# Neighbourhood attention: the products with v take the context's part first and the second head first

## Chip, cores and metric

The kernel runs on one core of one Trainium2 chip. The metric is device time of one execution in microseconds (us); three executions of the kernel before gave 3345.22, 3346.32 and 3348.22 us, median 3346.32. A second, profiled execution gives the trace from which every other time here is read.

## Reference

The program is a trunk of two layers over 1024 latent tokens (a grid of 16 rows by 64 columns) and 256 context tokens, width 1024. Layer 0 is a recurrent and a convolutional mixer, then an MLP. Layer 1, the one that is changed, is neighbourhood attention with 16 heads of width 64, then an MLP. For each grid row of queries:

```python
s_lat = jnp.einsum('bhqd,bhkd->bhqk', q_r, k_blk).astype(f32) + bias.astype(f32)
s_lat = jnp.where(blk_mask, s_lat, -jnp.inf)
s_ctx = jnp.einsum('bhqd,bhkd->bhqk', q_r, kc).astype(f32)
p = jax.nn.softmax(jnp.concatenate([s_lat, s_ctx], axis=-1), axis=-1).astype(v.dtype)
return (jnp.einsum('bhqk,bhkd->bhqd', p[..., :nk], v_blk)
        + jnp.einsum('bhqk,bhkd->bhqd', p[..., nk:], vc))
```

One softmax runs over the window's keys and all context keys; its weights are multiplied with the window's v and with the context's v, and the two products are added.

## The kernel before

Layer 1 works through eight **head pairs** (hp 0 to 7). `natten_proj` projects a pair's q, k and v from the normed activations: long chains of 128x512 products (L177 to L179, tiles psg), a sum of squares per head on TensorE (L902, tile psn), and a normalisation on ACT and DVE (tiles n). `natten_attn` then does the pair's attention in four **column blocks** (`cb`), and in each block for both heads (`hh`):

1. Scores: for each of two halves of the rows (`rb`) a product with the context's keys into the tile `pc` and one with the window's keys into a tile `p_`, each split into a high and a low part (L978, L979, tiles psf). One head needs three PSUM tiles of tag "f".
2. Softmax: DVE takes the maximum over the context part (L982), adds the bias `TM` and finishes the maximum (L984, twice), negates it (L986); ACT exponentiates (L989, L990, twice); DVE adds and inverts the sums (L96 st, L992) and scales (L994, twice).
3. Transposes of the weights on TensorE (L999 for each half's window part, L1006 for the context part) into one PSUM tile of tag "m", each evacuated before the next may start: L999 by ACT into tiles `s` (L1001), L1006 by DVE into a tile `pc` in SBUF (L1008).
4. When both heads are there, twenty products with v into one PSUM tile `po` (L1014 with the window's v `Vw`, L1018 with the context's `Vc`). Head 0 writes partitions 0 to 63 and head 1 partitions 64 to 127, so each uses half of the array's columns ("128*64" in the trace, where other products are "128*128"). `po` is copied out by ACT (L1192) and stored.

Buffers are few, which matters for the order. PSUM has three banks for tag "f" (scores and `po`), three for "g" (projections), one for "m" and one for "n":

```python
PS3 = dict(g=3, f=3, m=1, n=1)
```

The low part of q, `Ql`, has three buffers for the two heads of two pairs, and the next pair's second one is cleared on GpSimd (L897) when the pair's first head has read its own for the last time:

```python
Ql = [mk(nl, [P, LAT], "Ql", 3, F32R) for _ in range(2)]
for hh in range(2):
    G.memset(Ql[hh][64 - 64 * hh:128 - 64 * hh].bitcast(F32), 0.0)
```

Nothing of the order on an engine is written by hand. A scheduler fixes it before the run: attention has a high priority (`na=500`), and the next pair's projection fills TensorE in between. On the chip each engine runs its list strictly in that order, so an instruction that has to wait holds up all that stand behind it. Products that add into the same tile keep the order of the program.

Of the kernel before, what the change touches and what calls it, by code (L numbers as in the profile page):

```python
# [27 lines left out]
def kernel(ctx: ExitStack, tc: tile.TileContext, A, out):  # L28
    nc = tc.nc
    V, S, T, G = nc.vector, nc.scalar, nc.tensor, nc.gpsimd  # L30
# [8 lines left out]
    def mk(pool, shape, tag, bufs, dt=F32):  # L39
        cnt[0] += 1  # L40
        return pool.tile(shape, dt, tag=tag, bufs=bufs, name=f"{tag}_{cnt[0]}")
# [18 lines left out]
    def pr(k):  # L60
        k = HP.get(k, k)
        return ExitStack() if k is None else tc.high_priority(k)
# [13 lines left out]
    def pt(shape, tag):  # L76
        cnt[0] += 1
        return psp[0].tile(shape, F32, tag=tag, bufs=psp[1][tag], name=f"ps{tag}_{cnt[0]}")
# [7 lines left out]
    def s2(shape=None):  # L86
        return mk(base, shape or [P, 512], "s2", 4)
# [10 lines left out]
    def add(o, a, b):  # L98
        return tt(o, a, b, ALU.add)
# [845 lines left out]
    def natten_attn(hp, qkv, ap_, nl, store):  # L945
        with pr("na"):
            Q, Ql, Kt, vT = qkv
            vl = vT[:, 0:LAT].rearrange("p (r c) -> p r c", c=64)

            def tokens(src, n, tag):  # L950

                ps = pt([P, 4, P], TV)
                for i in range(n):
                    T.transpose(ps[:, i], src[:, i * P:(i + 1) * P], ident)
                o = mk(ap_, [P, n, P], tag, 2)
                S.copy(o, ps[:, :n])
                return o

            Vc = tokens(vT[:, LAT:NT], 2, "Vc")
            for cb in range(4):  # L960
                ct = (0, 1, 1, 2)[cb]
                vs = mk(ap_, [P, 512], "vs", 1)
                G.tensor_copy(vs.rearrange("p (r c) -> p r c", c=32), vl[:, :, KC0[cb]:KC0[cb] + 32])
                Vw = tokens(vs, 4, "Vw")
                pT = []
                for hh in range(2):
                    TM = mk(nl, [P, 2, 384], "TM", 2)
                    nc.gpsimd.dma_start(TM, A["rpbT"][2 * hp + hh, ct])
                    kl = Kt[hh][:, 0:LAT].rearrange("p (r c) -> p r c", c=64)
                    pc = pt([P, 2, CTX], "f")  # L970
                    st = mk(ap_, [P, 8], "st", 6)
                    pw, pe = [], []
                    for rb in range(2):
                        c0 = rb * 512 + cb * P
                        p_ = pt([P, 512], "f")
                        for o, kx in ((pc[:, rb], Kt[hh][:, LAT:NT]),
                                      (p_[:, :384], kl[:, 4 * rb:4 * rb + 12, KC0[cb]:KC0[cb] + 32])):
                            T.matmul(o, Q[hh][:, c0:c0 + P], kx, start=True, stop=False)  # L978
                            T.matmul(o, Ql[hh][:, c0:c0 + P], kx, start=False, stop=True)  # L979
                        pw.append(p_)  # L980
                        pe.append(mk(ap_, [P, 640], "pe", 4))
                    V.tensor_reduce(out=st[:, 0:2], in_=pc, axis=AX.X, op=ALU.max)  # L982
                    for rb in range(2):
                        V.tensor_tensor_reduce(out=pe[rb][:, 0:384], in0=pw[rb][:, :384], in1=TM[:, rb], scale=1.0, scalar=st[:, rb:rb + 1],  # L984
                                               op0=ALU.add, op1=ALU.max, accum_out=st[:, 2 + rb:3 + rb])
                    V.tensor_scalar(out=st[:, 2:4], in0=st[:, 2:4], scalar1=-1.0, scalar2=None, op0=ALU.mult)  # L986
                    for rb in range(2):
                        e = pe[rb]
                        S.activation(e[:, 0:384], e[:, 0:384], AF.Exp, bias=st[:, 2 + rb:3 + rb], accum_out=st[:, 4 + rb:5 + rb])  # L989
                        S.activation(e[:, 384:640], pc[:, rb], AF.Exp, bias=st[:, 2 + rb:3 + rb], accum_out=st[:, 6 + rb:7 + rb])  # L990
                    add(st[:, 4:6], st[:, 4:6], st[:, 6:8])
                    V.reciprocal(st[:, 4:6], st[:, 4:6])  # L992
                    for rb in range(2):
                        V.tensor_scalar(out=pe[rb], in0=pe[rb], scalar1=st[:, 4 + rb:5 + rb], scalar2=None, op0=ALU.mult)  # L994
                    tw = []
                    for rb in range(2):
                        ps = pt([P, 4, P], (TA, TB)[rb])
                        for j in range(3):
                            T.transpose(ps[:, j], pe[rb][:, j * P:(j + 1) * P], ident)  # L999
                        w_ = s2([P, 3, P])  # L1000
                        S.copy(w_, ps[:, 0:3])  # L1001
                        tw.append(w_)
                    ps = pt([P, 2, 2, P], TC)
                    for rb in range(2):
                        for j in range(2):
                            T.transpose(ps[:, j, rb], pe[rb][:, 384 + j * P:512 + j * P], ident)  # L1006
                    tc_ = mk(ap_, [P, 2, 2, P], "pc", 2)
                    V.tensor_copy(tc_, ps)  # L1008
                    pT.append((tw, tc_))
                po = pt([P, 2, P], PO)  # L1010
                for rb in range(2):
                    for j in range(3):
                        for hh in range(2):
                            T.matmul(po[64 * hh:64 * hh + 64, rb], Vw[:, rb + j, 64 * hh:64 * hh + 64],  # L1014
                                     pT[hh][0][rb][:, j], start=(j == 0), stop=False)
                    for j in range(2):
                        for hh in range(2):
                            T.matmul(po[64 * hh:64 * hh + 64, rb], Vc[:, j, 64 * hh:64 * hh + 64],  # L1018
                                     pT[hh][1][:, j, rb], start=False, stop=(j == 1))
                store(cb, po)  # L1020


# [162 lines left out]
    with tc.tile_pool(name="nl", bufs=1, reuse_waits="tile") as nl, \  # L1185
# [3 lines left out]
        def store(hp):  # L1189
            def f(cb, po):  # L1190
                o = mk(nl, [P, 2, P], "o", 1)
                S.copy(o, po)  # L1192
                nc.gpsimd.dma_start(od[hp, :, :, cb], o)
            return f

        for hp in range(7):
            natten_attn(hp, natten_proj(hp, h, na, nl, cst, *([OR] if hp == 0 else [])), na, nl, store(hp))
# [4 lines left out]
        def direct(cb, po):  # L1202
            for g in range(2):
                hi, lo = blkd(g, 7)
                split(hi[:, cb], lo[:, cb], po[:, g].rearrange("p (r q) -> p r q", q=16))

        natten_attn(7, qkv, na, nl, direct)
        xg = [mk(hpool[0], [P, 8, 512], "h2", 1)]
        nc.sync.dma_start(xg[0], xs[:, :, 0:512])
# [158 lines left out]
```

## Time and profile before

| | us |
|---|---|
| median of three executions | 3346.32 |
| profiled execution, whole | 3341.84 |
| span of its trace | 3340.1 |
| attention of layer 1 in the trace, first product with v to last | 1958.1 to 2561.2 |

The page of the profile gives each engine's busy time and the chain of work that ended last. The timeline lists an engine's instructions in order of time: start, length, engine, line, tile, how many were merged, and in brackets how long the engine stood idle before them and for what. A product's length includes the passage through the array, which overlaps the next product, so the cost of one is the distance between starts. A product with v is recorded as two passes: 640 products stand as 768 + 512 records.

### The profile page before, as it was taken

Reading aid. Unit: us, or ns where it says so; the run is one execution under the profiler, and the core shown is the slowest. Engines: PE = TensorE matmul, PEld = TensorE weight load, DVE = VectorE, ACT = ScalarE, POOL = GpSimd, SP = SyncE. Lnnn points to the kernel's source line nnn. Section 1 sums busy time; section 2 is a strip of 40 time slices with the busy share of each in tenths; the row PEclk is TensorE's granted clock in tenths of the full one; section 3 lists DMA queues with packets and bytes.
Section 4 is the critical chain, followed back from the end, with each engine's and each line's share of the span. In section 5 each row is a group of like instructions: output and inputs, shape, how many; then the busy total and the mean of one; then the engine's idle time right before and its main releaser. Section 6 shows DMA issues by size and latency. Waiting matters only on the chain.

```text
span 3340.1 us, 45203 instructions
## 1 busy us (share of the span) xinstructions
PE 3232.4 (97%) x18044; PEld 2637.5 (79%) x18044; DVE 2056.8 (62%) x3790; ACT 1200.4 (36%) x2539; POOL 96.5 (3%) x160
## 2 busy tenths in 40 slices
PE   7799999999999999999999999999999999999999
PEld 4678887778877888888888777777777788888887
DVE  4958997556684444544445877666666754455454
ACT  5742221343442212111121576666664422121111
POOL 0000000000000000000000011111110000000000
PEclk9899999999999999999999999999999999999999
DMA  6432224776522212121111221222234111111111
GB/s 208 163 110 67 81 73 146 231 241 208 189 97 95 70 57 89 57 89 64 51 45 32 79 69 59 70 64 70 67 96 144 65 62 46 49 51 47 48 45 70
DMA packets 140876, 306.11 MB, mean 92 GB/s; under 512 B 12497, under 2 KB 74057, under 8 KB 139258
## 3 DMA queue, kind: packets, MB, share of 16 engines
q1 hardware_dynamic: 131018, 266.60, 24.5%
q0 software_dynamic: 6464, 28.84, 2.8%
q10 hardware_dynamic: 3184, 7.78, 0.7%
q8 instruction: 142, 2.33, 0.3%
q14 instruction: 68, 0.56, 0.1%
HBM read 255.93 MB, written 43.05 MB: 90 GB/s over the span
## 4 chain that ended last, share of the span: by engine, by line
PE 77%; DVE 8%; DMA 3%; ACT 2%; issue 1%; SPq 0%; ACTq 0%; DVEq 0%
PE psg L177 13%; PE psg L178 13%; PE psg L179 13%; PE psf L313 8%; PE psf L312 8%; PE psf L314 8%; DMA wm<-in_w_mod 3%; PE psf L1014 2%; PE psm L999 1%; DVE b L96 1%; PE psf L978 1%; PE psf L979 1%; DVE n L108 1%; DVE q L96 1%; PE psf L1018 1%; PE psm L218 1%
## 5 line engine op out<-in xcount | busy, mean ns | idle before, releaser
L177 PE MATMUL psg<-h,wh 128*128 128x512 f32 (+1 forms) x2728 | 1014.8, 372 | 13.5 <-ACT h L289 7.1
L179 PE MATMUL psg<-h,wl 128*128 128x512 f32 (+1 forms) x2728 | 1003.9, 368 | 5.7 <-DVE wl L113 5.4
L178 PE MATMUL psg<-h,wh 128*128 128x512 f32 (+1 forms) x2728 | 1007.9, 370 | 1.0 <-DVE h L108 0.9
L177 PEld LDWEIGHTS psg<-h,wh 128*128 128x128 f32 x2728 | 516.5, 189 | 109.4 <-issue 17.3
L179 PEld LDWEIGHTS psg<-h,wl 128*128 128x128 f32 x2728 | 516.2, 189 | 93.4 <-DVE wl L113 10.6
L178 PEld LDWEIGHTS psg<-h,wh 128*128 128x128 f32 x2728 | 516.3, 189 | 91.7 <-issue 14.2
L108 DVE SCALAR_TENSOR_TENSOR x<-psf,modT,x 128x512 f32<-128x512 f32 (+1 forms) x512 | 347.1, 683 | 218.8 <-PE psf L314 218.7
L313 PE MATMUL psf<-al,w2h 128*128 128x512 f32 (+1 forms) x1280 | 471.6, 369 | 0.6 <-DVE al L113 0.6
L314 PE MATMUL psf<-ah,w2l 128*128 128x512 f32 (+1 forms) x1280 | 470.9, 368 | 0.0
L312 PE MATMUL psf<-ah,w2h 128*128 128x512 f32 (+1 forms) x1280 | 468.6, 369 | 0.1
L112 ACT CAST w2h<-w2r 128x1024 fp32r<-128x1024 f32 x64 | 67.3, 1051 | 765.9 <-PE psf L313 595.9
L113 DVE TENSOR_TENSOR wl<-wr,wh 128x1024 fp32r<-128x1024 f32 (+2 forms) x144 | 172.9, 1200 | 213.3 <-ACT wh L112 212.7
L312 PEld LDWEIGHTS psf<-ah,w2h 128*128 128x128 f32 x1280 | 240.4, 188 | 44.4 <-ACT ah L112 2.6
L313 PEld LDWEIGHTS psf<-al,w2h 128*128 128x128 f32 x1280 | 241.2, 189 | 43.3 <-DVE al L113 2.3
L314 PEld LDWEIGHTS psf<-ah,w2l 128*128 128x128 f32 x1280 | 241.2, 188 | 40.4 <-issue 0.5
L112 ACT CAST wh<-wr 128x1024 fp32r<-128x1024 f32 (+2 forms) x144 | 148.4, 1031 | 249.2 <-PE psg L178 207.6
L108 DVE SCALAR_TENSOR_TENSOR rr<-psg,rr 128x512 f32<-128x512 f32 x160 | 101.3, 633 | 176.6 <-ACT rr L301 176.6
L113 DVE TENSOR_TENSOR w2l<-w2r,w2h 128x1024 fp32r<-128x1024 f32 x64 | 78.2, 1222 | 151.6 <-ACT w2h L112 149.9
L301 ACT ACTIVATE rr<-psg 128x512 f32<-128x512 f32 x160 | 88.0, 550 | 194.7 <-PE psg L179 193.3
L113 DVE TENSOR_TENSOR al<-rr,ah 128x512 fp32r<-128x512 f32 x160 | 101.8, 636 | 84.1 <-ACT ah L112 84.1
L112 ACT CAST ah<-rr 128x512 fp32r<-128x512 f32 x160 | 92.4, 578 | 170.0 <-DVE rr L108 170.0
L108 DVE SCALAR_TENSOR_TENSOR h<-psf,modT,h 128x512 f32<-128x512 f32 x128 | 94.2, 747 | 44.2 <-PE psf L314 44.2
(286 smaller groups left out, 4046.2 us busy)
## 6 DMA issues: line engine op xcount, KB each, us to landing
wm<-in_w_mod SPq DMA_DIRECT2D x96, 512.0 KB
wr<-in_w SPq DMA_DIRECT2D x64, 512.0 KB
w2r<-in_w SPq DMA_DIRECT2D x64, 512.0 KB
big<-d SPq DMA_DIRECT2D x39, 640.0 KB
TM<-in_rpbT POOLq DMA_DIRECT2D x64, 384.0 KB, 3.4
wr<-in_w_in SPq DMA_DIRECT2D x29, 512.0 KB
wr<-in_w_qkv SPq DMA_DIRECT2D x24, 512.0 KB
d<-b SPq DMA_DIRECT2D x8, 1280.0 KB
```

The lines of the kernel that those rows point to most:

```text
L96: return (e or V).tensor_tensor(out=o, in0=a, in1=b, op=op)
L108: return V.scalar_tensor_tensor(out=o, in0=a, scalar=s, in1=b, op0=op0, op1=op1)
L112: S.copy(hi, x)
L113: (e or V).tensor_tensor(out=lo, in0=x, in1=hi.bitcast(F32), op=ALU.subtract)
L177: T.matmul(ps[:M, :n], hi[:, k, :M], hh[g][:, k, :n], start=(i == 0), stop=False)
L178: T.matmul(ps[:M, :n], hi[:, k, :M], hl[g][:, k, :n], start=False, stop=False)
L179: T.matmul(ps[:M, :n], lo[:, k, :M], hh[g][:, k, :n], start=False, stop=(i == len(ks) - 1))
L301: S.activation(r[:, :n], ps[:, :n], AF.Relu)
L312: T.matmul(ps[:, :n], w2h[:, d], ah[g], start=(i == 0), stop=False)
L313: T.matmul(ps[:, :n], w2h[:, d], al[g], start=False, stop=False)
L314: T.matmul(ps[:, :n], w2l[:, d], ah[g], start=False, stop=(i == 1))
L1014: T.matmul(po[64 * hh:64 * hh + 64, rb], Vw[:, rb + j, 64 * hh:64 * hh + 64], pT[hh][0][rb][:, j], start=(j == 0), stop=False)
```

## The change

The two loops of each `rb` change places, and the heads are visited as (1, 0):

```diff
                 for rb in range(2):
+                    for j in range(2):
+                        for hh in (1, 0):
+                            T.matmul(po[64 * hh:64 * hh + 64, rb], Vc[:, j, 64 * hh:64 * hh + 64],
+                                     pT[hh][1][:, j, rb], start=(j == 0), stop=False)
                     for j in range(3):
-                        for hh in range(2):
+                        for hh in (1, 0):
                             T.matmul(po[64 * hh:64 * hh + 64, rb], Vw[:, rb + j, 64 * hh:64 * hh + 64],
-                                     pT[hh][0][rb][:, j], start=(j == 0), stop=False)
-                    for j in range(2):
-                        for hh in range(2):
-                            T.matmul(po[64 * hh:64 * hh + 64, rb], Vc[:, j, 64 * hh:64 * hh + 64],
-                                     pT[hh][1][:, j, rb], start=False, stop=(j == 1))
+                                     pT[hh][0][rb][:, j], start=False, stop=(j == 2))
```

The same twenty products per block remain. The context's products are L1014 in the kernel after and L1018 in the kernel before, the window's the other way round. The first product now needs the second head's transposed context weights, the last tile that a block makes.

The scheduler's order changes with it, on TensorE from the first block of hp 0 to the end of hp 7. The first place is TensorE at the third block of hp 5 (scores of the block after it are psf_20735 and psf_20737). Before, the first product with v stands alone, between the first head's transposes and the next block's scores:

```order
L999 MATMUL psm_20640<-ident,pe_20621 128x128 x3
L1014 MATMUL psf_20700<-s_3713_20638,Vw_20604 64x128
L978 MATMUL psf_20735<-KK_20025,Q_20019 128x256
L979 MATMUL psf_20735<-KK_20025,Ql_20021 128x256
L978 MATMUL psf_20735<-KK_20025,Q_20019 128x256
L979 MATMUL psf_20735<-KK_20025,Ql_20021 128x256
L179 MATMUL psg_20960<-h_1650_8777,wl_20957 128x512
L177 MATMUL psg_20960<-h_1650_8777,wh_20956 128x512
L1006 MATMUL psm_20646<-ident,pe_20615 128x128 x2
```

Five more of that block's products follow with one of the context's behind the second head's L999, and thirteen more behind its L1006. After, the block's twenty stand together directly behind the second head's L1006; these are the first of them:

```order
L1006 MATMUL psm_20693<-ident,pe_20662 128x128 x2
L1006 MATMUL psm_20693<-ident,pe_20668 128x128 x2
L1014 MATMUL psf_20700<-pc_20698,Vc_20341 64x128
L1014 MATMUL psf_20700<-pc_20651,Vc_20341 64x128
L1014 MATMUL psf_20700<-pc_20698,Vc_20341 64x128
L1014 MATMUL psf_20700<-pc_20651,Vc_20341 64x128
L1018 MATMUL psf_20700<-s_3726_20685,Vw_20604 64x128
```

What moved: in each of the 32 blocks three runs of 1, 6 and 13 products became one run of 20, and the scores of the next block, which stood between those runs, now stand behind the run.

The second place is TensorE right behind that run, in the fourth block of the same pair. After, all sixteen score products of both heads come first (the last eight of them are shown), then one L902 and the first head's transposes, and only then a projection product:

```order
L978 MATMUL psf_20782<-KK_20026,Q_20020 128x256
L979 MATMUL psf_20782<-KK_20026,Ql_20022 128x256
L978 MATMUL psf_20784<-KK_20026,Q_20020 128x384
L979 MATMUL psf_20784<-KK_20026,Ql_20022 128x384
L978 MATMUL psf_20790<-KK_20026,Q_20020 128x384
L979 MATMUL psf_20790<-KK_20026,Ql_20022 128x384
L902 MATMUL psn_21029<-n_3793_21027,bd_8340 128x512
L999 MATMUL psm_20761<-ident,pe_20742 128x128 x3
L999 MATMUL psm_20767<-ident,pe_20748 128x128 x3
L177 MATMUL psg_21092<-h_1650_8777,wh_21088 128x512
```

Before, the first head's scores of that block had been issued a block earlier, and projection products stand in front of its transposes:

```order
L978 MATMUL psf_20790<-KK_20026,Q_20020 128x384
L979 MATMUL psf_20790<-KK_20026,Ql_20022 128x384
L179 MATMUL psg_21002<-h_1652_8779,wl_20957 128x512
L177 MATMUL psg_21002<-h_1652_8779,wh_20956 128x512
L178 MATMUL psg_21002<-h_1653_8780,wh_20956 128x512
L179 MATMUL psg_21002<-h_1652_8779,wl_20957 128x512
L177 MATMUL psg_21002<-h_1652_8779,wh_20956 128x512
L178 MATMUL psg_21002<-h_1653_8780,wh_20956 128x512
L999 MATMUL psm_20761<-ident,pe_20742 128x128 x3
```

What moved: the scores of the first head went from before the third block's products with v to behind them, and six projection products that stood between the scores and the transposes are gone from there. The same piece of order, with other tile numbers, stands in hp 0 to hp 6.

The third place is DVE at that same fourth block, where st_20736 is the first head's statistics and Ql_20854 the next pair's second `Ql`. After:

```order
L982 TENSOR_REDUCE st_20736<-psf_20735 128x2
L96 TENSOR_TENSOR Ql_20854<-n_3778_20896,Q_20852 64x512
L984 ISA pe_20742,st_20736<-psf_20737,TM_20733,st_20736 128x384
L984 ISA st_20736 128x1
L984 ISA pe_20748,st_20736<-psf_20743,TM_20733,st_20736 128x384
L984 ISA st_20736 128x1
L96 TENSOR_TENSOR Ql_20854<-n_3783_20940,Q_20852 64x512
L986 TENSOR_SCALAR st_20736<-st_20736 128x2
```

Before, both L984 stand ahead of the first write of Ql_20854, with other work between:

```order
L984 ISA pe_20748,st_20736<-psf_20743,TM_20733,st_20736 128x384
L984 ISA st_20736 128x1
L96 TENSOR_TENSOR Ql_20854<-n_3778_20896,Q_20852 64x512
L986 TENSOR_SCALAR st_20736<-st_20736 128x2
L108 SCALAR_TENSOR_TENSOR n_3783_20940<-psg_20910,gain_8344,n_3783_20940 128x512
```

What moved: the write of Ql_20854, which must wait for GpSimd's clearing and so for the first head's last score product, went ahead of the two L984 of that head.

## Prediction

> **What bounds the kernel now.** I read the page first, then the stage of the attention by windows, then its timeline.
>
> ```profile
> PE 3232.4 (97%) x18044; PEld 2637.5 (79%) x18044; DVE 2056.8 (62%) x3790; ACT 1200.4 (36%) x2539; POOL 96.5 (3%) x160
> ...
> core 0: us, PE busy (x) PEld busy (x) DVE busy (x) ACT busy (x) POOL busy (x), PEclk, DMA share, GB/s
> ...
> 1995.00:2003.00 8.00, 5.44 (x39) 3.40 (x33) 6.79 (x17) 6.09 (x17) 2.63 (x4) 1.00 0.40 126
> 2003.00:2500.00 497.00, 493.45 (x3290) 387.99 (x3290) 342.07 (x767) 327.34 (x820) 73.40 (x111) 1.00 0.22 68
> 2500.00:2562.00 62.00, 58.34 (x401) 44.76 (x402) 42.84 (x98) 34.25 (x91) 4.01 (x7) 0.94 0.48 155
> ```
>
> TensorE (PE) is the bound: in the 497 us of hp 1 to 6 it stands idle for 3.55 us. DVE and ACT are busy for 69% and 66% of it and set nothing there, because projection products always stand between an attention step and the next one that needs its result. Two stretches are different: in hp 0 (1995 to 2003) a third of PE's time is idle, and hp 7 loses 3.7 us. So the change matters in two ways only: what it takes from PE's own work, and whether PE still has something to do while a softmax runs.
>
> **What it removes: changes of the array's shape.** The products with v use half of the columns. Around a run of them the timeline of PE shows a gap:
>
> ```profile
> 2286.95 0.55 PE L999 MATMUL psm<-ident,pe 128*128 128x128 f32 x3
> 2287.43 0.76 PE L1014 MATMUL psf<-s,Vw 128*64 128x128 f32 x9
> 2287.92 0.27 PE L1018 MATMUL psf<-pc,Vc 128*64 128x128 f32 x1
> 2288.03 0.27 PE L1014 MATMUL psf<-s,Vw 128*64 128x128 f32 x1
> 2288.03 0.27 PE L1018 MATMUL psf<-pc,Vc 128*64 128x128 f32 x1
> 2288.24 0.39 PE L979 MATMUL psf<-KK,Ql 128*128 128x256 f32 x1
> 2288.46 0.40 PE L177 MATMUL psg<-h,wh 128*128 128x512 f32 x1
> ...
> 2289.83 0.34 PE L978 MATMUL psf<-KK,Q 128*128 128x384 f32 x1
> 2290.00 0.34 PE L979 MATMUL psf<-KK,Ql 128*128 128x384 f32 x1
> ...
> 2291.95 0.66 PE L954 MATMUL psm<-ident,vs 128*128 128x128 f32 x4
> ...
> 2295.27 0.55 PE L999 MATMUL psm<-ident,pe 128*128 128x128 f32 x3 [0.19 <-ACT s L1001]
> 2295.75 0.43 PE L1014 MATMUL psf<-s,Vw 128*64 128x128 f32 x2
> 2296.11 0.39 PE L978 MATMUL psf<-KK,Q 128*128 128x256 f32 x1
> 2296.34 0.28 PE L979 MATMUL psf<-KK,Ql 128*128 128x256 f32 x1
> 2296.45 0.28 PE L978 MATMUL psf<-KK,Q 128*128 128x256 f32 x1
> ```
>
> Passes of the two heads run side by side: pairs start 0.11 apart (2287.92, 2288.03). The run of 6: the third L999 (a single pass is 0.27 long) started at 2286.95 + 0.55 - 0.27 = 2287.23, and at full width the next product would have started 0.11 later, at 2287.34; L979 starts at 2288.24, which is 0.90, and its own step is 0.22 where it is 0.11 at 2296.34, so the run costs 1.00. The lone product likewise: from 2295.55 + 0.11 to 2296.11 is 0.45, and L978's step is 0.23 instead of 0.12: 0.56. The run of 13: from 2290.00 + 0.18 (step of a 384-wide product, 2289.83 to 2290.00) to 2291.95 is 1.77. Together 3.33 us a block. One run of 20 is the run of 6 with 14 more pairs: 0.90 + 14 x 0.11 = 2.44, and it ends on L954 as the run of 13 does. Saved: 0.89 us a block, **28.5 us** in 32 blocks, if PE is never made to wait. The context before the window, and head 1 before head 0, cost nothing by themselves: the heads still alternate and the passes are the same.
>
> The Trainium skill, "TensorEngine Tiling (Array Packing)", section "Tiling Modes", says that changing the tiling mode drains TensorE. The gaps above agree; by that rule alone the change would be worth its 64 saved changes of mode, which is the first rival below.
>
> **What it moves: the next block's scores.** The twenty products now come when both heads are done, and the next block's scores stand behind them (second place of the order above). Before, the first head's softmax of the next block ran under the second head's transposes and the runs of 6 and 13. Now all of a block's chain begins behind the previous block's products, and what covers it is only what the order put in between. In the first block of each pair plenty of projection stands there; in the fourth of hp 0 to 6 there is only one L902. The price is read from the same steps of the trace before:
>
> ```profile
> 1990.32 0.52 PE L999 MATMUL psm<-ident,pe 128*128 128x128 f32 x3 [0.46 <-DVE pe L994]
> 1991.41 0.55 PE L999 MATMUL psm<-ident,pe 128*128 128x128 f32 x3 [0.57 <-ACT s L1001]
> ...
> 1992.70 0.66 PE L1006 MATMUL psm<-ident,pe 128*128 128x128 f32 x4
> ...
> 1994.14 0.54 PE L1018 MATMUL psf<-pc,Vc 128*64 128x128 f32 x5 [0.43 <-DVE pc L1008]
> ...
> 1998.66 0.44 PE L978 MATMUL psf<-KK,Q 128*128 128x384 f32 x1 [1.27 <-ACT pe L990]
> ...
> 1999.15 1.12 PE L902 MATMUL psn<-n,bd 128*128 128x512 f32 x2
> 2000.85 0.52 PE L999 MATMUL psm<-ident,pe 128*128 128x128 f32 x3 [0.57 <-DVE pe L994]
> 2002.08 0.55 PE L999 MATMUL psm<-ident,pe 128*128 128x128 f32 x3 [0.72 <-ACT s L1001]
> ...
> 1994.00 0.61 DVE L984 CUSTOM_DVE_ANT_0 pe<-psf,TM,st 128x384 f32<-128x384 f32 x1
> ...
> 1994.65 0.69 DVE L96 TENSOR_TENSOR Ql<-n,Q 64x512 fp32r<-64x512 f32 x1
> 1995.37 0.17 DVE L986 TENSOR_SCALAR st<-st 128x2 f32<-128x2 f32 x1
> ...
> 1998.90 0.61 DVE L984 CUSTOM_DVE_ANT_0 pe<-psf,TM,st 128x384 f32<-128x384 f32 x1
> ...
> 1996.25 0.35 ACT L1192 COPY o<-psf 128x256 f32<-128x256 f32 x1
> 1996.51 0.59 ACT L956 COPY Vw<-psm 128x512 f32<-128x512 f32 x1
> 1996.99 0.48 ACT L990 ACTIVATE pe<-psf,st 128x256 f32<-128x256 f32 x1
> ...
> 2302.14 0.34 PE L979 MATMUL psf<-KK,Ql 128*128 128x384 f32 x1
> ...
> 2302.55 0.95 POOL L897 MEMSET Ql<- 64x1024 f32 x1 [8.04 <-PE psf L979]
> ...
> 2303.42 0.69 DVE L96 TENSOR_TENSOR Ql<-n,Q 64x512 fp32r<-64x512 f32 x1
> ...
> L932 ACT CAST Q<-n 64x512 fp32r<-64x512 f32 x56 | 34.6, 618 | 0.7
> ...
> TM<-in_rpbT POOLq DMA_DIRECT2D x64, 384.0 KB, 3.4
> ```
>
> *Fourth block, hp 0 to 6.* Time 0 is its first score. The first head's eight products (four of 0.12, four of 0.18) put its last L979 at 1.0; it ends at 1.34. GpSimd's clearing of `Ql` starts 0.07 after such an end (2302.48 to 2302.55), at 1.4, and DVE's write of `Ql` 0.87 after that (2303.42), at 2.3. In the new order of DVE that write stands ahead of both L984: they start at 3.0 and 3.6, and L986 follows the second by 1.37 (1994.00 to 1995.37, a `Ql` write between them as here): 4.95. The last score product needs the bank of `pc`, which ACT frees after both exponentials: before, 3.29 behind L986 (1995.37 to 1998.66), of which two copies took 0.74 (1996.25 to 1996.99) that now stand earlier: 2.55, so 7.5. From it to the first L999 is 2.19 (1998.66 to 2000.85), with one more L108 on DVE now (0.6) and 0.2 less queueing: 10.1. The second L999 starts 1.23 later and ends its work 0.33 behind: 11.7. PE's own work in that stretch is sixteen scores (2.4), L902 (0.9) and six transposes (0.65), 3.9. **PE waits 7.8 us.**
>
> *Run of 20 right behind L1006 in the third block.* Between the last transpose (1993.09) and the product that needs DVE's copy (1994.14) lie 1.05; nothing covers them now but the transpose's own 0.1 and the gap already counted, 0.1: 0.85.
>
> *Second and third block.* Projection products cover most, but the last score product waits for `pc` again. In the second, four casts of q on ACT (0.62 each, L932), in front of them in the new order, hold the exponentials to 4.4, so it starts at 6.7 and the first L999 at 8.9, where PE has 7.4 us of rows; in the third 5.8 and 8.0 against 6.9. So 1.5 and 1.1.
>
> That makes 11.3 a pair. What PE waits there today I estimate at 0.9 a pair: the 3.55 us above are 0.6 for each of six, and part of each wait hides under the length of the product before it. Extra: 10.4 x 6 = **62 us** in hp 1 to 6.
>
> *hp 0* has less projection to put in. Third block: no projection at all. Without the `Ql` writes the first L999 comes at about 8.8; four hand-overs of the one transposing bank at about 1.1 (1.09 between the starts at 1990.32 and 1991.41, 1.23 at 2000.85 and 2002.08) and DVE's copies put the twenty at 15.2, where PE has 4.6 of work: 10.6. Its second block adds 1.2, and four bare hand-overs and the copy at its end 4.4; the fourth 7.8. Together 24, of which some 4 are there today (0.46, 0.57, 0.43, 1.27, 0.57 and 0.72 above): **20 us**.
>
> *hp 7* runs its first block with no projection already; the scores that stood between its transposes leave, three hand-overs of 0.8 are bare: 2.4 us. SP's queue only swaps weight loads near the end; GpSimd's bias loads keep a block of lead. I cost both at nothing: the transfers finish several us before use, and an uncovered one (`TM`) would add its landing time of 3.4 us once a pair.
>
> **Sum.** -28.5 + 62 + 20 + 2.4 = +56. On the profiled execution, 3341.84 + 56 = 3398; the median shown lies 4.5 higher, so **3402 us**. Bounds of the unknown terms: the fourth block's wait, if DVE did not have to stand behind `Ql`, would be 5.3 (1.9 less for the first L984, 0.6 for the L108), and up to 9 if the casts queue there too; with the second and third between 0.3 and 2 each, a pair gives 6.7 to 13 before today's 0.9. hp 0 may give 12 to 26. That is +21 to +73 for all, and some 10 more if projection products come late as well.
>
> **Rivals.** *Faster:* the 64 changes of shape decide and the waits stay as they are, some 6 us more: 3346 - 28.5 + 6 = 3324. For it speaks that PE is full and the waits before are 0.9 a pair; against it that those waits were short because of products that the new order has moved away. It decides if the fourth block needs under some 5 us from first score to second transpose; the rows give 11.7. *Cancelled:* the fourth block waits only what hp 0's does today (1.27 + 0.57 + 0.72 = 2.6), a pair 4.5: -28.5 + 3.6 x 6 + 12 + 2 = +7, 3353; against it, today that block's first head starts a block earlier. *Steeper:* later attention also delays the normalisation of the next projection, so that fillers wait: +85, 3431. That the order doesn't hold is no rival: TensorE's list has 32 runs of 20.
>
> **How the numbers follow.** Forecast 0.73, steeper 0.10, cancelled 0.07, faster 0.10. About 0.2% is what a measurement tells from no change (6.7 us), and the cancelled case stands for that. The range takes the forecast's bounds, part of the steeper case and what lies between cancelled and forecast: 3358 to 3432. Faster 0.10, same 0.07, slower 0.83.
>
> **What would show it.** In the profile after: runs of 20 of about 2.4 us; in each fourth block of hp 0 to 6 a last L978 that waits for ACT's L990 and an L999 that waits for DVE's L994, 6 to 8 us together; PE idle in the stage up by some 80 us; the clearing of `Ql` inside the first head's softmax. I am wrong if PE's idle time in hp 1 to 6 stays under 30 us, or if a run of 20 costs over 3 us.

## The result, and the profile after

The changed kernel takes 3408.26 us (median of 5 runs, 3402.76 to 3412.94), the kernel before 3345.22 us in the runs beside it: a ratio of 1.0186, 95% interval 1.0174 to 1.0199. It is 63 us slower; forecast was 3402 us, range 3358 to 3432. The profiled execution took 3412.65 us, with a span of 3410.9. One execution of the last experiment below took 5177 us, at a granted clock of 0.63, and is left out of that run's figures.

The first view answers to the two shown of before: the page's line of busy times, and the stage of the attention by windows (us, then busy time of PE, PEld, DVE, ACT and POOL, the granted clock, the DMA share, GB/s).

```profile
PE 3255.1 (95%) x18044; PEld 2655.7 (78%) x18044; DVE 2055.4 (60%) x3790; ACT 1206.1 (35%) x2539; POOL 97.9 (3%) x160
...
2003.00:2500.00 497.00, 456.57 (x2969) 355.00 (x2970) 305.05 (x693) 295.47 (x734) 69.00 (x103) 0.92 0.20 60
```

In the same 497 us PE now stands idle for 40.4 us where it was 3.55, and its granted clock is 0.92 where it was 1.00. The second number stood in no term of the forecast. Over the whole span PE is busy for 22.7 us *longer* than before (3255.1 against 3232.4), although the changes of shape that the prediction meant to save are gone. So time was lost in two ways: PE waited, and when it worked it worked more slowly.

The next view is the timeline of PE in one block, the fourth of hp 1 (start, length, line, operands, and in brackets the idle time before it with what ended it):

```profile
2107.97 0.36 PE L978 MATMUL psf<-KK,Q 128*128 128x256 f32 x1
...
2109.07 0.34 PE L979 MATMUL psf<-KK,Ql 128*128 128x384 f32 x1
2111.22 0.39 PE L978 MATMUL psf<-KK,Q 128*128 128x256 f32 x1 [1.80 <-DVE st L984]
...
2114.41 0.69 PE L978 MATMUL psf<-KK,Q 128*128 128x384 f32 x1 [2.03 <-DVE st L984]
...
2115.47 2.08 PE L902 MATMUL psn<-n,bd 128*128 128x512 f32 x2
2117.41 0.88 PE L999 MATMUL psm<-ident,pe 128*128 128x128 f32 x3
2119.35 0.90 PE L999 MATMUL psm<-ident,pe 128*128 128x128 f32 x3 [1.07 <-ACT s L1001]
2119.91 0.78 PE L177 MATMUL psg<-h,wh 128*128 128x512 f32 x1
2120.48 0.63 PE L178 MATMUL psg<-h,wh 128*128 128x512 f32 x1
2120.91 0.63 PE L179 MATMUL psg<-h,wl 128*128 128x512 f32 x1
...
2123.40 0.39 PE L177 MATMUL psg<-h,wh 128*128 128x512 f32 x1
2123.63 0.39 PE L178 MATMUL psg<-h,wh 128*128 128x512 f32 x1
```

The second head's scores wait 1.80 for a bank that DVE's L984 reads, and its last score 2.03 more. Then products take about twice their time: the two L902 are 2.08 long (1.12 before, at 1999.15), a step of a projection product is 0.43 (2120.48 to 2120.91) where it is 0.23 from 2123.40 on. The windows of this place say the same by the granted clock. The first is the whole stretch from the block's first score to the projection product behind its transposes, the second the part of it, and beyond, in which the clock is at half:

```profile
2107.97:2119.91 11.94, 6.99 (x28) 4.02 (x26) 8.83 (x22) 5.65 (x16) 3.61 (x5) 0.71 0.32 113
2113.07:2123.31 10.24, 7.79 (x20) 4.88 (x21) 5.82 (x17) 7.63 (x23) 1.43 (x2) 0.50 0.23 77
```

The clock falls inside the second wait, 1.3 us before it ends, and stays at half for 10.24 us.

What the waits wait for, from the timelines of GpSimd and DVE at that place:

```profile
2109.48 0.94 POOL L897 MEMSET Ql<- 64x1024 f32 x1 [0.46 <-PE psf L979]
...
2109.82 0.69 DVE L96 TENSOR_TENSOR Ql<-n,Q 64x512 fp32r<-64x512 f32 x1
2110.54 0.62 DVE L984 CUSTOM_DVE_ANT_0 pe<-psf,TM,st 128x384 f32<-128x384 f32 x1
...
2111.08 0.61 DVE L984 CUSTOM_DVE_ANT_0 pe<-psf,TM,st 128x384 f32<-128x384 f32 x1
...
2111.73 0.69 DVE L96 TENSOR_TENSOR Ql<-n,Q 64x512 fp32r<-64x512 f32 x1
2112.45 0.17 DVE L986 TENSOR_SCALAR st<-st 128x2 f32<-128x2 f32 x1
2112.53 0.68 DVE L982 TENSOR_REDUCE st<-psf 128x2 f32<-128x512 f32 x1
2113.13 0.68 DVE L96 TENSOR_TENSOR n<-n 128x512 f32<-128x512 f32 x1
2113.73 0.61 DVE L984 CUSTOM_DVE_ANT_0 pe<-psf,TM,st 128x384 f32<-128x384 f32 x1
```

The first wait ends when the first head's first L984 has read its scores (2110.54 + 0.62 = 2111.16, and PE goes on at 2111.22). The second ends with the *second* head's first L984 (2113.73 + 0.61 = 2114.34, PE at 2114.41): by the releaser that the trace names, the last score takes the bank that this L984 frees. DVE comes to it late: two writes of the next pair's `Ql` (2109.82 and 2111.73, 0.69 each) and a step of a projection's normalisation (2113.13) stand in its row ahead of it.

Where the 70.8 us between the two profiled executions lie can be read off PE's timeline, by the start of the first score (L978) and of the last product with v of each pair. The fourth column takes out what only moved: the trace has 5, 30 and 30 projection products more inside hp 0, hp 1 and hp 7 and 65 fewer after the attention, 14.9 us in all, 0.23 for each 512 columns (some are 256 wide).

| part, us | before | after | difference | without moved projection | forecast |
|---|---|---|---|---|---|
| up to the first score | 1947.6 | 1958.3 | +10.7 | +10.7 | 0 |
| hp 0 | 64.5 | 87.4 | +22.9 | +21.7 | +20 - 3.6 |
| hp 1 to 6 | 466.8 | 514.7 | +47.9 | +42.2 | +62.4 - 21.4 |
| hp 7 | 82.3 | 89.6 | +7.3 | -0.7 | +2.4 - 3.6 |
| after it, to TensorE's last product | 774.8 | 756.8 | -18.0 | -3.1 | 0 |

The first row is not the change's: up to there both programs give TensorE the same list, and other kernels below with that list reach the first score at 1951 to 1956. Without it +60 us are left, against a forecast of +56.

### The profile page after: what moved, and what is told of

It is laid out like the page before. It is cut to its first block, busy times and chain, and to the rows that moved or that the text cites. A ratio compares the mean times of both kernels' runs of the same rounds, so it can differ in the third digit from the quotient of the medians.

```text
span 3410.9 us, 45179 instructions
## 1 busy us (share of the span) xinstructions
PE 3255.1 (95%) x18044; PEld 2655.7 (78%) x18044; DVE 2055.4 (60%) x3790; ACT 1206.1 (35%) x2539; POOL 97.9 (3%) x160
## 5 line engine op out<-in xcount | busy, mean ns | idle before, releaser
L177 PE MATMUL psg<-h,wh 128*128 128x512 f32 (+1 forms) x2728 | 1019.7, 374 | 12.6 <-ACT h L289 6.9
L177 PEld LDWEIGHTS psg<-h,wh 128*128 128x128 f32 x2728 | 519.1, 190 | 106.3 <-issue 16.0
```

The lines of the kernel that those rows point to most:

```text
L177: T.matmul(ps[:M, :n], hi[:, k, :M], hh[g][:, k, :n], start=(i == 0), stop=False)
```

## The experiments

Two explanations were to be told apart first. The products with v write into one of the three PSUM banks (`psf`) that the scores also use, and the order of TensorE suggests that the pool gives its banks out in the order of the program: until the first product with v has asked for its bank, no score of the next block can have one. **Theory 1 (the bank):** the harm is only that this request now comes last in the block. **Theory 2:** the long run at the block's end is itself the harm, because of where it stands or of what comes first in it.

**The two halves of the change alone.**

```diff
-                        for hh in range(2):
+                        for hh in (1, 0):
```

(in both loops; the window stays first.)

> The second head first, the window before the context as it was: TensorE's list has 32 runs of 6 and 32 of 14. Theory 1 (the bank): in the changed kernel all 20 products share one bank of the pool of three that the scores use, and that bank is first asked for by the context's product of head 1, at the end of the block, so that the next block's scores stand behind the run; here the window's product of head 1 asks for it ahead of the last four transposes, and six scores stand ahead of the 14. Then the waits of the fourth blocks (6 us a pair in the changed kernel) fall under 2 us a pair and what is left is two changes of shape a block fewer: 3345 - 16 + 4 = 3333 us (3325 to 3342). Theory 2 (a long run at the end is the harm, whatever stands ahead of it): 14 of 20 products still come at the end, 3385 us.

Measured: 3376.49 us, 1.0077 of before (1.0062 to 1.0092). Between the two: 43 us above what Theory 1 expected, 9 below what Theory 2 did.

The other half leaves head 0 first and puts the context's loop ahead of the window's (arguments shortened):

```diff
+                    for j in range(2):
+                        for hh in range(2):
+                            T.matmul(po[...], Vc[...], pT[hh][1][:, j, rb], start=(j == 0), stop=False)
                     for j in range(3):
                         for hh in range(2):
```

> The context before the window, head 0 first: 32 runs of 1 and 32 of 19. Theory 1 (the bank): the single product of head 0 asks for the bank, the next block's scores go ahead of the 19; saved are two changes of shape a block, some 0.4 us x 32 = 12, waits under 2 us a pair: 3335 us (3325 to 3345). Theory 2 (a long run at the end is the harm, or the context's products that wait for DVE's copy): 19 of 20 products are where the changed kernel has them, 3400 us (3390 to 3410).

Measured: 3353.3 us, 1.0008 of before (0.9999 to 1.0018). That is no measurable difference from before, and 55 us faster than the whole change, although 19 of 20 products are where the change has them. Theory 2 falls here: a run of 19 at the end with the context first costs nothing that can be measured. Theory 1's range (3325 to 3345) is missed too, by 8 us. The stage by windows shows PE full again (idle 4.05 of 497 us, clock 0.99):

```profile
2003.00:2500.00 497.00, 492.95 (x3307) 387.68 (x3306) 337.64 (x768) 326.42 (x815) 75.60 (x113) 0.99 0.22 67
```

A pair takes 78.2 us there where it took 78.9, so the saved changes of shape do arrive in part; hp 0 and 1 together take 14 us more than before (150.9 against 136.9), part of it projection products that moved into them. What the rest is was not measured.

Where the 26 us of the heads alone come from is seen in the waits of PE in the whole attention, 1940 to 2660 (line waited for, us in all, times, longest):

```profile
PE psn L902 <- ACT n L900: 11.1, 9, 1.7
PE psm L999 <- ACT s L1001: 7.1, 12, 0.7
PE psm L1006 <- ACT s L1001: 5.4, 8, 0.9
```

Six of a fourth block's sixteen score products do go ahead of the run of 14, but now the transposes of fourth blocks stand bare and L902 waits for ACT's square. A pair takes 81.6 us in hp 2 to 4 (83.4 and 83.7 in hp 5 and 6, to which the half clock below comes back). So an early request for the bank isn't all that is needed; what then stands in the fourth block counts as well. Why the scheduler puts no projection there was not found out.

**A bank of its own.** The products get one of the projection's three banks:

```diff
+    psum(g=2, f=3, m=1, n=1, o=1)
...
-                po = pt([P, 2, P], PO)
+                po = pt([P, 2, P], "o")
```

> The changed kernel, with a PSUM bank of its own for the products with v (taken from the projection's three, which become two): runs of 20 stay, but the next block's scores no longer stand behind them. Theory 1 (the bank): the fourth blocks' waits go and the shape changes are all that is left, 3345 - 28 = 3317, plus what the projection loses with two banks (see the next run), 3312 to 3335 us; the granted clock in the stage is back at 1.00. Theory 2 (the long run): still 3395 to 3410 us.

> Control for the run above: the kernel before, with the same banks (two for the projection, one for the products with v). Both theories: 3340 to 3360 us; Theory 1 says that the run above is 20 to 30 us faster than this one, Theory 2 that it is 50 to 60 slower.

Measured: 3387.77 us (1.0111, 1.0093 to 1.0128) and 3395.21 us (1.0134, 1.0118 to 1.0149). Both lie above their ranges, the first by 53 us and the control by 35: two banks are too few for the projection. The control's waits in the whole attention (1940 to 2660):

```profile
PE psg L177 <- DVE n L96: 13.9, 8, 2.0
PE psn L902 <- ACT n L900: 9.0, 7, 1.3
```

Between the two kernels the sign is Theory 1's (82.2 against 83.7 us a pair, the changed products 7 us faster in all where Theory 2 wanted 50 slower), the size is a third of what was expected. As a test it was poor, because it took away something else that the stage needs.

**The bank of the transposes.** This bank is used one tile after another anyway, and the products need DVE's copy of its last tile before they can start. One word changes (`PO` is "f", the scores' banks):

```diff
-                po = pt([P, 2, P], PO)
+                po = pt([P, 2, P], "m")
```

> The changed kernel, with the products with v put into the bank of the transposes instead of one of the three banks that the scores use; the projection keeps its three. TensorE's list has 31 runs of 20 (one in hp 0 is cut in three), the next block's scores stand between the transposes and right behind the run again, and projection products stand in all fourth blocks of hp 1 to 6. Theory 1 (the harm is only that the products' late first use of the scores' bank holds the next block's scores back): waits of hp 1 to 6 under 1.5 us a pair, a pair takes 75.5 to 76.5 us (78.9 before, 85.6 in the changed kernel), in all 3345 - 20 = 3325 us (3315 to 3335). Theory 2 (a run of 20 at the end is itself the harm): 3390 us or more. A rival in between: the single bank of the transposes now also waits for ACT's copy of the result before the next block's values can be transposed, 0.4 us or so a block uncovered, 3338.

> The kernel before (window first, head 0 first) with the same bank. Its products have to wait for the bank until DVE has copied the context's transposes out, so TensorE's list has 31 runs of 20 here too and differs from the run above only in which operand comes first inside a run. If context first and head 1 first cost nothing by themselves (as the prediction has it), the same time as the run above within 0.2%; if they do cost, the run above is slower by the part that is due to them.

Measured: **3327.12 us, 0.9948 of before (0.9935 to 0.996)** with the changed products, and 3332.53 us, 0.996 (0.9947 to 0.9972) with those of before. The two agree within their intervals: which operand and which head comes first in a run costs nothing that can be measured. And the change of bank alone turns the changed kernel's 3408 us into 3327, with the run of 20 where it was. That is the case for Theory 1, and the version that beats both kernels. The order on TensorE shows the step between: in the fourth block of hp 2, 14 of the 16 score products start before the third block's first product with v, where in the changed kernel all 16 start behind its last and with the context alone eight follow the lone first product. The stage by windows, and the end of a block's run in the timeline of PE:

```profile
2003.00:2500.00 497.00, 488.47 (x3324) 389.47 (x3325) 341.31 (x775) 326.66 (x830) 73.84 (x114) 0.99 0.24 74
```

```profile
2146.80 0.82 PE L1018 MATMUL psm<-s,Vw 128*64 128x128 f32 x12
2147.55 0.44 PE L978 MATMUL psf<-KK,Q 128*128 128x384 f32 x1
...
2148.01 0.40 PE L179 MATMUL psg<-h,wl 128*128 128x512 f32 x1
...
2148.99 0.63 PE L954 MATMUL psm<-ident,vs 128*128 128x128 f32 x4
```

Only the last score pair of the fourth block, its second head's, stands behind the run; the rest was done before it, and the next transposes find their bank free after projection products. A pair takes 77.0 us, 1.9 less than before and 8.5 less than in the changed kernel; 75.5 to 76.5 were expected.

**The half clock.** To see whether it comes from the idle time, the waits of the changed kernel were filled with work whose result nobody needs. First the first wait only:

```diff
+                    if cb == 3 and hh == 0:
+                        pd = pt([P, 512], "m")
...
+                    if cb == 3 and hh == 0:
+                        for _ in range(10):
+                            T.matmul(pd[:, :384], Q[0][:, 0:P], kl[:, 0:12, 0:32], start=True, stop=True)
                     V.tensor_reduce(out=st[:, 0:2], in_=pc, axis=AX.X, op=ALU.max)
```

> The changed kernel with ten more score products (128x384, 0.18 us each, into an unused bank, result not used) in every fourth block of each pair, between the scores of the first and of the second head, where TensorE waits 1.8 us; the order is the same otherwise. Clock theory: the half clock that stands for some 8 us behind the two waits comes from the idle time, and with the first wait filled it is gone: 3.5 to 4 us a pair in hp 0 to 6, 3408 - 25 = 3383 us (3378 to 3392). Rival: the clock has another cause, or the second wait of 2.0 us is enough for it: 3405 to 3415 us.

The bank is that of the transposes ("m"), which nothing uses at that moment. Measured: 3410.52 us, 1.0194 (1.0178 to 1.0209): no gain, a pair takes 85.4 us instead of 85.5. The half clock stayed, 6.83 us long instead of 10.24. Ahead of it lie the second wait of 2.02 and two of 0.43:

```profile
2108.43 0.45 PE L980 MATMUL psf<-KK,Q 128*128 128x384 f32 x1 [2.02 <-DVE st L992]
...
2109.49 1.13 PE L902 MATMUL psn<-n,bd 128*128 128x512 f32 x2 [0.43 <-ACT n L900]
2111.05 0.84 PE L1007 MATMUL psm<-ident,pe 128*128 128x128 f32 x3 [0.43 <-DVE pe L1002]
2112.46 0.90 PE L1007 MATMUL psm<-ident,pe 128*128 128x128 f32 x3 [0.57 <-ACT s L1009]
...
2113.59 0.63 PE L178 MATMUL psg<-h,wh 128*128 128x512 f32 x1
2114.02 0.63 PE L179 MATMUL psg<-h,wl 128*128 128x512 f32 x1
```

```profile
2111.09:2117.92 6.83, 6.26 (x20) 4.88 (x21) 3.22 (x9) 5.63 (x15) 0.00 (x0) 0.50 0.20 60
```

(Line numbers are 2 higher here at the scores and 8 higher behind them: L980 is L978, L992 is L984, L1007 is L999.) L902, at 2109.49, still runs at full rate; the step at 2113.59 is 0.43, and the wait of 0.57 comes when the clock has fallen already. Then both waits:

```diff
+                        for _ in range(6 if cb == 3 and hh == 1 and rb == 0 else 0):
+                            T.matmul(o, Q[hh][:, c0:c0 + P], kx, start=True, stop=False)
+                            T.matmul(o, Ql[hh][:, c0:c0 + P], kx, start=False, stop=True)
                         pw.append(p_)
```

> As the run with one wait filled, and the second wait of the fourth block (2.0 us, in front of the last score product of 384 columns) filled too: the score product of 384 columns before it is computed seven times instead of once (2.1 us more, same result). The order is the same otherwise. Clock theory: with both long waits gone the granted clock stays at 1.00, so L902 and the projection products behind the fourth block run at 0.23 instead of 0.43 us a step; in the changed kernel that was 2.4 to 3 us a pair, so 3408 - 7 x 2.5 = 3390 us (3385 to 3398). Rival: the slow clock costs nothing (it lies beside waits anyway), or has another cause and stays: 3404 to 3414 us.

Measured: 3394.6 us (three executions, 3393.72 to 3396.99), 1.0138 (1.0118 to 1.0158): less than the changed kernel's 1.0186, the intervals apart. TensorE does some 4.1 us of useless work (1.97 from 2101.75 on, and twelve products of 0.18) in each fourth block of its pairs, and the kernel is 14 us faster. First the stage by windows, then the timeline of the fourth block of hp 1, as above:

```profile
2003.00:2500.00 497.00, 478.57 (x3200) 378.50 (x3202) 313.99 (x708) 302.82 (x750) 71.89 (x104) 0.99 0.20 61
```

```profile
2100.48 0.36 PE L980 MATMUL psf<-KK,Q 128*128 128x256 f32 x1
...
2107.49 0.45 PE L980 MATMUL psf<-KK,Q 128*128 128x384 f32 x1 [0.45 <-ACT pe L998]
...
2107.97 1.13 PE L902 MATMUL psn<-n,bd 128*128 128x512 f32 x2
2109.68 0.52 PE L1007 MATMUL psm<-ident,pe 128*128 128x128 f32 x3 [0.58 <-DVE pe L1002]
2110.90 0.55 PE L1007 MATMUL psm<-ident,pe 128*128 128x128 f32 x3 [0.71 <-ACT s L1009]
2111.20 0.47 PE L177 MATMUL psg<-h,wh 128*128 128x512 f32 x1
...
2113.21 0.40 PE L177 MATMUL psg<-h,wh 128*128 128x512 f32 x1
```

From the first L177 behind the block to the one six projection products and four L1006 later it takes 2.01 here (2111.20 to 2113.21) and 3.49 in the changed kernel (2119.91 to 2123.40). The pair takes 83.6 instead of 85.5 us. So idle time makes the clock fall, and by this run the fall costs about 1.9 us a pair net. It is not a clean subtraction: the last score now waits for ACT's L990 (L998 here), for 0.45, and fill and remaining waits together are 1.0 us a pair longer than the waits were (6.8 against 5.7).

The run with the heads alone swapped gives the same price without any fill. TensorE's list is the same in hp 2 to hp 5, and so are its waits to within 0.4 us, but of these four only hp 5 has a fall of the clock. Here are hp 4 and hp 5:

```profile
2272.50:2354.00 81.50, 77.81 (x528) 60.59 (x524) 52.73 (x122) 51.51 (x130) 11.63 (x18) 1.00 0.22 65
2354.00:2437.50 83.50, 80.16 (x530) 62.41 (x526) 53.05 (x122) 51.98 (x130) 11.63 (x18) 0.96 0.22 64
```

The pair with the fall takes 83.4 us where the other takes 81.6, although PE is idle for 0.4 us less in it.

## Why the prediction was right, point by point

**The total: right, and in part by luck.** These are the windows of hp 1 to 6 (before, after) and of hp 0 (before, after):

```profile
2012.00:2479.00 467.00, 464.75 (x3116) 364.65 (x3113) 318.95 (x720) 306.23 (x768) 70.78 (x107) 1.00 0.22 67
2046.00:2560.00 514.00, 480.27 (x3136) 374.59 (x3138) 319.54 (x726) 313.50 (x774) 71.61 (x107) 0.94 0.21 62
1947.60:2012.00 64.40, 60.27 (x430) 46.62 (x430) 47.64 (x116) 46.72 (x119) 9.64 (x15) 1.00 0.23 73
1958.30:2045.70 87.40, 71.26 (x436) 54.58 (x435) 50.13 (x118) 47.77 (x120) 9.63 (x15) 0.82 0.17 54
```

The mechanism that the prediction named is there: the next block's scores stand behind the run and the fourth block lies bare. But in hp 1 to 6 PE's idle time rose by 31 us (2.3 to 33.7) where waits of 62 were forecast, and its busy time by 16 (464.8 to 480.3), or 10 without the moved projection, where 21 less was forecast. Two terms are off by some 31 us each, and they cancel: +42 by the table, +41 forecast. The points below take this apart as far as the runs allow.

**Shape changes, -28.5: right in the rows, about half of it in the time.** In one steady pair of the changed kernel PE's 160 rows of products with v, from each start to the next, take 9.34 us where they took 11.37, and the steps into and out of the runs shrink besides; a run of 20 costs 2.43 by the prediction's own way of reckoning (2.44 forecast). In the kernel with the other bank the V rows and the transposes ahead of them together take 3.36 less a pair (13.80 against 17.16), where 3.56 were forecast; 1.2 of it go to the projection products' steps and more to others, so that 1.9 a pair reach the time, some 15 of the 28.5 us. The first rival (the faster case, and with it the Trainium skill's rule from "TensorEngine Tiling (Array Packing)", section "Tiling Modes") names a saving that is there; it decides only where nothing has to wait for it, as with the other bank: 18 us less than before, where the rival had 22. (What the prediction counts as 64 changes of shape are 64 runs fewer, each of which began and ended with a change.)

**The fourth block, 7.8: right in size, not in its parts.** From the first score at 2107.97, forecast against measured: clearing of `Ql` 1.4 and 1.51; first L984 3.0 and 2.57; L986 4.95 and 4.48; last score 7.5 and 6.44; first L999 10.1 and 9.44; second L999 11.33 and 11.38; end 11.7 and 11.94. With 3.9 of PE's own work that is a loss of 8.0. But by the first window of this place shown above PE is busy for 6.99 of the 11.94 and idle for 4.95. The idle time lies in front of the second head's first score (1.80), of its last (2.03) and of the second L999 (1.07, for ACT's L1001). The sign to look for was another: 6 to 8 us in front of a last score that waits for ACT's L990 and an L999 that waits for DVE's L994. The releaser of the last score is DVE's L984 of the second head. The other 3.1 us are longer rows of PE, which ran at half clock from 2113.07 on. With both waits filled the same stretch takes 10.72 at full clock (2100.48 to 2111.20), 6.8 more than 3.9: by that run the term is 1.0 too large, and the half clock made up for it.

**Run of 20 behind L1006, 0.85: right.** PE waits 0.8 for DVE's copy once a pair, in the third block (last line):

```profile
PE psf L978 <- DVE st L984: 3.8, 2, 2.0
PE psm L999 <- ACT s L1001: 1.1, 1, 1.1
PE psf L1014 <- DVE pc L1008: 0.8, 1, 0.8
```

**Second and third block, 1.5 + 1.1: wrong.** The three lines just shown are all waits that the profile lists in hp 2 (2131.4 to 2216.9); none lies in the second block, and in the third only L1014's. The projection products left there covered the softmax. This step was over-sized by 2.6 us a pair.

**The clock: missing.** The prediction had PE at full rate whenever it worked. It ran at half rate around the end of every fourth block, 1.9 us a pair net by the run with both waits filled, some 11 us in hp 1 to 6. That is also one reason why the sign to look for, PE idle up by some 80 us, was not met: the idle time rose from 107.7 to 155.8 us (span less busy), by 48, and the 33.7 us in hp 1 to 6 only just pass the 30 below which the theory was to count as wrong. A product that takes twice its time counts as busy. How the rest of the two cancelling errors divides between the clock, the saving that went to other steps, and waits that hide under the recorded length of the product before them was not measured.

**hp 0, +20, and hp 7, +2.4: right in sign, hp 0 by 5 us too small.** Net of the saved shape changes 16.4 and -1.2 were forecast; 21.7 and -0.7 were measured without the moved projection. In hp 0 the split is off as in the pairs behind it: PE's idle time rose by 12 us (4.1 to 16.1) where 20 were forecast, and its busy time by 11 (60.3 to 71.3), with the granted clock at 0.82 instead of 1.00.

**The cause behind the scores' new place: not given.** The prediction read the place of the next block's scores from TensorE's order and priced it. That they stand there because the products take a bank from the scores' pool, and ask for it late, came out of the experiments. With that the price could have been removed, not only foreseen.

**The other rivals.** *Cancelled* needed a fourth block that waits 2.6; it loses 8.0, of which 4.95 are idle. *Steeper*, fillers that wait: L902 waits for ACT in hardly any place of the changed kernel, but does so for 11.1 us with the heads alone swapped, so the mechanism is real and fell on a variant. (The range's upper bound leaves the 0.85 out of its sum: 9 + 0.85 + 4 is 13.9 a pair, not 13, which would have raised it by 5 us.)

## What to carry to other kernels

Before a step is moved, ask which pool its result's buffer comes from and who asks next: a later first use can hold back work that needs nothing from it. A bank that is released by the very copy that the moved products wait for cost next to nothing to share here (PE idle for 8.5 of 497 us in the stage, 3.55 before), and turned a loss of 1.9% into a gain of 0.5%. Where waits of 2 us appear on TensorE, allow for a slower stretch behind them as well, and read the granted clock by stage, since the busy share hides it. A total that fits is no proof of its terms: read idle and busy time apart.

## What the hardware showed that was not expected

The granted clock fell to one half after waits that are short: 1.80 us and the first 0.7 of another of 2.03, with about 1 us of products between (changed kernel, 2113.07); 2.02, 0.43 and 0.43 within 4.7 us (first wait filled, 2111.09); or a single one of 1.68 (heads alone, hp 5, 2424.16). The same list with a wait of 1.7 in the same place left it at 1.00 in hp 2 to 4 of that run, and so did waits of 1.27, 0.57 and 0.72 in hp 0 of the kernel before. In the changed kernel it was at half for 10.24 us (2113.07 to 2123.31), with the first wait filled for 6.83.

The Trainium skill, "TensorE: Matmul & The Clock Gate", section "HAM oscillation — how this bites in real kernels", gives as the rule that no gap of PE should be longer than about 3.4 us; the half rate agrees (0.43 against 0.23 us a step), the length doesn't: no wait at these places was over 2.1 us. And since equal waits let the clock fall in one pair and not in the next, the waits of a place alone don't decide. What else does was not measured.
